# Hybrid attention layer on one core: the latent heads' gate projection as seven half-block products with tokens as rows

## The chip, the core and the metric

One core of a Trainium2 chip runs the whole layer in one launch. The time is the device time of an execution in microseconds. TensorE (PE) multiplies, VectorE (DVE) and ScalarE (ACT) work elementwise, GpSimd (POOL) and SyncE (SP) mostly issue DMAs here.

## The reference

512 tokens of width 2048, all in float32. The parts that matter:

```python
h = _rms_norm(x, g_pre)
proj = h @ w_in                      # split into q_lat, kv_lat, k_rope_raw, gate_mla, fq, fk, fv, f_logit, gate_fox
o_mla = _mla_branch(q_lat, kv_lat, k_rope_raw, g_q, w_uq, g_kv, w_ukv, cos, sin) * jax.nn.silu(gate_mla)
o_fox = _fox_branch(fq, fk, fv, f_logit, b_forget) * jax.nn.silu(gate_fox)
o = jnp.concatenate([o_mla, o_fox], axis=-1) @ w_out
return x + _rms_norm(o, g_post)
```

There are 8 latent (MLA) heads and 8 forgetting (fox) heads of width 128. gate_mla is the product of the normed x (512 x 2048) with a 2048 x 1024 block of w_in; it is this product that the change makes in another way.

## The kernel before

**Arithmetic.** Every operand of a product is split into a high and a low part, and `mm3` (L128 to 131) makes three matmuls of them: high x high (L129), high x low or low x high (L130, L131). x is turned at the start, so that its 16 blocks of 128 columns lie with columns on the partitions and 512 tokens in the row (`hh`, `hl`). The factor 1/rms of each token comes in later, as a row (`rrow`) or a column (`rcol`).

**Weights.** They come in chunks of 128 x 1024 numbers (512 KB). `load` (L205) issues a chunk's DMA on SP into one of three `raw` buffers. `divide` (L226) makes the parts: a cast on ACT (L232, tile whi) and a subtraction on DVE (L233, wlo), three buffers each. `chunk(i)` (L243) asks for loads four chunks ahead and divides two ahead. The list of chunks is in the order of use.

**Order of the work.** Projections run on TensorE chunk by chunk; a projection stage with weights as the stationary operand and 512 tokens moving is `proj_T` (L429), one with tokens as rows is `proj_V` (L442). After each block of 128 columns of x (a k step) `pump` takes a step from the queue `todo`: heads' scores, softmax, turns (L555) and values, operand splits and so on are worked off between projections. `drain` empties that queue. An order of each engine's instructions follows from this and from a scheduler, except for the first projection.

**Sums of weight blocks.** The output projection is already made, for each of two column pairs of 512, as seven products of half-sized blocks instead of eight (p1, p2, p4, q6, g5, g7, g3). These need sums of w_out's blocks (t4 to t7). `add_blocks` (L301) makes one with DMAs alone: a tiny mark DMA (L303), which waits for a divided chunk and so sets the time, a copy into DRAM on SP's queue (L305), and an accumulating DMA on POOL's queue (L306). The 32 sums are in `bg`; `behind` (L424) issues one every 8 k steps as soon as the first heads are done. The products also need sums of the heads' outputs: `operand_steps` (L853) makes and splits them (L867 on DVE, then L120 and L121), `put_away` (L896) writes six operands of each of two pairs to DRAM through POOL, but for a11 and a12, which stay, and `fetch` (L902) reads them back on SP in the output stage.

**Stages.** First forgetting pair, three more forgetting pairs (each with q, k, v, gate projections and the attention of the pair before in `todo`), the rotary tables in between; latents (loop L914, 10 blocks, times `rrow` by L920); latent gate (L976 to 994: four `proj_T` over 16 k steps, with `gate_of` L594: product with rrow L597, Tanh L598, product L599), in which the latents' norms are also made (`latent_squares` L926, `latent_scale` L939, whose row is made by TensorE at L408) and their parts split (`part_latents` L970); the MLA heads (loop L1000); the output stage (`product` L1130, from L1188).

A step of the products in the output stage, operand block stationary and weights moving:

```python
mm3(
    o[t], ah, al, hi[:, j, :], lo[:, j, :], first and kk == 0, last and kk == 7,
    skip_group_check=True,
)
```

Of the kernel before, what the change touches and what calls it, by code (L numbers as in the profile page):

```python
# [12 lines left out]
F32 = mybir.dt.float32  # L13
# [50 lines left out]
def tile_hybrid_layer(  # L64
# [26 lines left out]
    tp = inner.enter_context(tc.tile_pool(name="tp", bufs=3))  # L91
# [89 lines left out]
    half, dummy = (cst.tile([P, 1], F32, name=n) for n in ("half", "dummy"))  # L181
# [54 lines left out]
    state = {"loaded": 0, "divided": 0}  # L236
# [30 lines left out]
    gml = [add_chunks(w_in, [(0, O_GM + 256 * p, 256)], NK, 4, 256) for p in range(4)]  # L267
# [30 lines left out]
    W = {}  # L298
    bg = deque()

    def add_blocks(to, first, second, mark):  # L301

        nc.sync.dma_start(to[0:1, 0:16], mark)  # L303
        to = to.rearrange("p (k c) -> p k c", k=2)
        nc.sync.dma_start(to, first)  # L305
        pool.dma_start(to, second, accum_op=ALU.add)  # L306

    for g in range(2):
        for name in ("t7", "t6", "t4", "t5"):

            W[name, g] = [dr.tile([P, 1040], F32, name=f"{name}{g}{j}")[:, :1024] for j in range(4)]
        for j in range(4):
            b11, b12, b21, b22 = (out_block(k[j], 2 * g + c) for k in (K1, K2) for c in range(2))
            t7, t6 = (W[n, g][j].rearrange("p (k c) -> p k c", k=2) for n in ("t7", "t6"))
            for name, first, second in (("t7", b12, b22), ("t5", b11, b12), ("t6", b11, t7), ("t4", b21, t6)):
                bg.append(lambda mark, x=(W[name, g][j], first, second): add_blocks(*x, mark))

    def add_plain(pairs, c):
        first = len(chunks)
        for pair in pairs:  # L320
            add_chunks(w_out, [(0, 512 * c, 512)], 2, 2, 512, out_rows(pair) // P)
        return range(first, len(chunks))

    def add_sums(name, g):
        first = len(chunks)
        chunks.extend((W[name, g][j], None, 0, 2, 512) for j in range(4))
        return range(first, len(chunks))

    outp = {}
    for name, g in (  # L330
        ("p1", 0), ("p1", 1), ("p2", 0), ("p4", 0), ("p4", 1), ("q6", 0), ("g5", 0), ("g7", 0),
        ("q6", 1), ("g5", 1), ("g7", 1), ("g3", 0), ("g3", 1), ("p2", 1),
    ):
        plain = {"p1": (K1, 0), "p2": (K2, 0), "g3": (K2, 1)}
        sums = {"p4": "t4", "q6": "t6", "g5": "t5", "g7": "t7"}
        if name in plain:
            outp[name, g] = add_plain(plain[name][0], 2 * g + plain[name][1])
        else:
            outp[name, g] = add_sums(sums[name], g)
# [79 lines left out]

    def drain():  # L420
        while todo:
            todo.popleft()()

    def behind(k, w):  # L424

        if done and bg and k % 8 == 0:
            bg.popleft()(w[0:1, 0, 0:16].bitcast(F32))

    def proj_T(rng, outs, kh, kl, rate=1):  # L429

        k = 0
        n_k = sum(chunks[i][3] for i in rng)
        for i in rng:
            hi, lo = chunk(i)
            for j in range(chunks[i][3]):
                for o, rows, pick in outs:
                    mm3(o[:rows, :], pick(hi, j), pick(lo, j), kh[k], kl[k], k == 0, k == n_k - 1)
                k += 1
                pump(rate)
                behind(k, hi)  # L440

    def proj_V(rng, banks, kh, kl, rate=1):  # L442
# [3 lines left out]
        for i in rng:  # L446
            hi, lo = chunk(i)
            for j in range(chunks[i][3]):
# [9 lines left out]
                behind(k, hi)  # L458
# [266 lines left out]

    done = []
# [62 lines left out]

    for p in range(4):  # L790
# [57 lines left out]

    HALF = S // 2
    TERMS = ("a11", "a12", "a22", "q6", "g5", "g7", "g3")  # L850
    oper = {n: [None] * 4 for n in TERMS}

    def operand_steps(j, names, raw_of, place, then=None):  # L853

        a = {}
        raw = {}

        def block(n):
            if not a:
                for h, pair in ((1, K1[j]), (2, K2[j])):  # L860
                    for t in range(2):
                        a[f"a{t + 1}{h}"] = o_of[pair][:, :, t * HALF : (t + 1) * HALF]
            return raw[n] if n in raw else a[n]

        def make(n, x, y):
            raw[n] = raw_of(f"r{n}{j}").rearrange("p (h c) -> p h c", h=2)
            dve.tensor_tensor(out=raw[n], in0=block(x), in1=block(y), op=ALU.subtract)  # L867

        def part(n):
            both = place(f"s{n}{j}").rearrange("p x (h c) -> p x h c", h=2)  # L870
            split_into(both[:, 0], both[:, 1], block(n))
            oper[n][j] = both
            if then is not None:
                then(n, j)

        steps = []
        for n in names:
            if n == "sums":
                steps += [
                    lambda: make("g5", "a21", "a22"),  # L880
                    lambda: make("q6", "a11", "g5"),
                    lambda: part("g5"),
                    lambda: part("q6"),
                    lambda: make("g3", "a12", "q6"),
                    lambda: part("g3"),
                    lambda: make("g7", "a21", "a11"),
                    lambda: part("g7"),
                ]
            else:
                steps.append(lambda n=n: part(n))  # L890
        return steps

    kept = ("a11", "a12")
    away = {}

    def put_away(n, j):  # L896

        if n not in kept:
            away[n, j] = dr.tile([P, 1024], F32, name=f"away{n}{j}")
            pool.dma_start(away[n, j].rearrange("p (x h c) -> p x h c", x=2, h=2), oper[n][j].bitcast(F32))  # L900

    def fetch(n, j):  # L902
        both = slot(f"b{n}{j}", F32R)
        nc.sync.dma_start(both.bitcast(F32), away[n, j].rearrange("p (x c) -> p x c", x=2))
        oper[n][j] = both.rearrange("p x (h c) -> p x h c", h=2)

    for j in (1, 0):
        todo.extend(
            operand_steps(j, ("a11", "a12", "a22", "sums"), tmp, lambda n: slot(n, F32R), put_away)
        )  # L910


    raw = []
    for p in range(5):  # L914
# [9 lines left out]
    LAT = (("q", 0, 6, QR), ("k", 6, 10, KVR))  # L924

    def latent_squares():  # L926
        accs = []
        both = slot("ls")
        for j, (name, lo, hi, _) in enumerate(LAT):
            acc = both[:, j, :]  # L930
            for i in range(lo, hi):
                dst = acc if i == lo else tmp(f"lq{name}{i}")
                act.square(dst, raw[i])
                if i > lo:
                    pool.tensor_tensor(out=acc, in0=acc, in1=dst, op=ALU.add)
# [363 lines left out]
```

## Time and profile before

| | us |
|---|---|
| median of 3 runs | 923.75 (923.0 to 925.07) |
| profiled execution | 921.93 |
| its span | 920.1 |
| TensorE busy / DVE / ACT / POOL | 908.7 / 557.2 / 379.2 / 62.1 |
| DMA moved | 152.14 MB, mean 165 GB/s |

A row of groups reads: line, engine, operation, result <- inputs, number of instructions, busy time, mean ns of one, idle time of the engine before them and what ended it. Timeline rows start with the start in us from the span's begin and the length. TensorE's matmuls overlap in their records, so the distance of their starts says more than their length. Windows give the busy time of each engine in a stretch, then the granted clock of TensorE, the share of the 16 DMA engines and GB/s.

### The profile page before, as it was taken

The numbers are of one execution on the slowest core, as the hardware profiler recorded it, in microseconds if no ns is written. First come the engines' busy times: TensorE is split into PE (matmuls) and PEld (weight loads), VectorE is DVE, ScalarE is ACT, GpSimd is POOL, SyncE is SP. The second block draws the span as 40 slices with busy tenths as digits, with TensorE's granted clock in tenths as the row PEclk, the third lists the DMA queues.
The fourth block names the chain that finished last, engine by engine and source line by source line (L and its number), as shares of the span: only waits on it lengthen the run. The fifth ranks groups of instructions, "written<-read, shape, count | busy, mean of one in ns | idle before, by whom it ended". The sixth has DMA issues, their size and how long they took to land.

```text
span 920.1 us, 11945 instructions
## 1 busy us (share of the span) xinstructions
PE 908.7 (99%) x4472; PEld 771.3 (84%) x4472; DVE 557.2 (61%) x970; ACT 379.2 (41%) x683; POOL 62.1 (7%) x74
## 2 busy tenths in 40 slices
PE   8999999999999999999999999999999999999996
PEld 7888888998889888888888888888888888888885
DVE  3478744447833744483742234957978895876686
ACT  5772432233422522242421134434444455644473
POOL 1000000000000000000211013000000000000022
PEclk9999999999999999999999999999999999999999
DMA  9343365876666766766998733223222146787768
GB/s 303 90 116 114 92 160 138 209 181 180 150 159 173 197 168 153 197 167 162 293 279 211 177 92 92 81 82 96 57 63 84 46 138 209 241 318 230 274 194 249
DMA packets 109214, 152.14 MB, mean 165 GB/s; under 512 B 14274, under 2 KB 74204, under 8 KB 109156
## 3 DMA queue, kind: packets, MB, share of 16 engines
q1 hardware_dynamic: 99172, 126.86, 44.3%
q0 software_dynamic: 9248, 24.12, 14.1%
q8 instruction: 35, 0.57, 0.2%
q10 hardware_dynamic: 736, 0.40, 0.2%
q14 instruction: 23, 0.19, 0.1%
HBM read 141.90 MB, written 43.01 MB: 201 GB/s over the span
## 4 chain that ended last, share of the span: by engine, by line
PE 97%; DVE 2%; ACT 0%; issue 0%; DVEq 0%; ACTq 0%
PE fv L490 4%; PE l L129 4%; PE l L130 4%; PE l L131 4%; PE fg L129 3%; PE fq L129 3%; PE fq L130 3%; PE fq L131 3%; PE fg L130 3%; PE fg L131 3%; PE gm L129 3%; PE fk L129 3%; PE gm L131 3%; PE fk L130 3%; PE gm L130 3%; PE fk L131 3%
## 5 line engine op out<-in xcount | busy, mean ns | idle before, releaser
L233 DVE TENSOR_TENSOR wlo<-raw,whi 128x1024 fp32r<-128x1024 f32 (+3 forms) x181 | 215.6, 1193 | 231.3 <-ACT whi L232 223.3
L232 ACT CAST whi<-raw 128x1024 fp32r<-128x1024 f32 (+3 forms) x181 | 184.1, 1018 | 352.9 <-PE l L130 65.4
L129 PE MATMUL l<-h,whi 128*128 128x512 f32 x160 | 63.2, 395 | 0.0
L131 PE MATMUL l<-h,wlo 128*128 128x512 f32 x160 | 62.4, 390 | 0.0
L130 PE MATMUL l<-h,whi 128*128 128x512 f32 x160 | 62.3, 390 | 0.0
L129 PE MATMUL fq<-h,whi 128*128 128x512 f32 x128 | 52.7, 412 | 0.0
L129 PE MATMUL fg<-h,whi 128*128 128x512 f32 x128 | 50.4, 394 | 0.0
L130 PE MATMUL fq<-h,whi 128*128 128x512 f32 x128 | 50.2, 392 | 0.0
L131 PE MATMUL fq<-h,wlo 128*128 128x512 f32 x128 | 50.2, 392 | 0.0
L129 PE MATMUL fk<-h,whi 128*128 128x512 f32 x128 | 50.1, 391 | 0.0
L130 PE MATMUL fg<-h,whi 128*128 128x512 f32 x128 | 50.0, 390 | 0.0
L131 PE MATMUL fg<-h,wlo 128*128 128x512 f32 x128 | 49.9, 390 | 0.0
L129 PE MATMUL gm<-h,whi 128*128 128x512 f32 x128 | 49.9, 390 | 0.0
L131 PE MATMUL fk<-h,wlo 128*128 128x512 f32 x128 | 49.8, 389 | 0.0
L131 PE MATMUL gm<-h,wlo 128*128 128x512 f32 x128 | 49.8, 389 | 0.0
L130 PE MATMUL gm<-h,whi 128*128 128x512 f32 x128 | 49.8, 389 | 0.0
L130 PE MATMUL fk<-h,whi 128*128 128x512 f32 x128 | 49.8, 389 | 0.0
L131 PE MATMUL fv<-whi,h 128*128 128x256 f32 (+1 forms) x128 | 39.5, 309 | 0.0
L130 PE MATMUL fv<-wlo,h 128*128 128x256 f32 (+1 forms) x128 | 39.5, 309 | 0.0
L129 PE MATMUL fv<-whi,h 128*128 128x256 f32 (+1 forms) x128 | 39.5, 309 | 0.0
L306 POOL DMA_DIRECT2D t<-in_w_out_dram x16 | 18.7, 1169 | 293.6 <-DMA t<-in_w_out_dram 285.4
L490 PE MATMUL fv<-whi,h 128*128 128x456 f32 x128 | 37.9, 380 | 0.0
(401 smaller groups left out, 2086.4 us busy)
## 6 DMA issues: line engine op xcount, KB each, us to landing
raw<-in_w_in_dram SPq DMA_DIRECT2D x88, 512.0 KB
t<-in_w_out_dram SPq DMA_DIRECT2D x32, 512.0 KB
raw<-t SPq DMA_DIRECT2D x32, 512.0 KB
raw<-in_w_out_dram SPq DMA_DIRECT2D x24, 512.0 KB
t<-in_w_out_dram POOLq DMA_DIRECT2D x16, 512.0 KB, 7.0
t<-t POOLq DMA_DIRECT2D x16, 512.0 KB, 6.3
raw<-in_w_ukv_dram SPq DMA_DIRECT2D x8, 512.0 KB
xa<-in_x_dram SPq DMA_DIRECT2D x7, 512.0 KB
```

Of the source, the lines that this page charges most:

```text
L129: pe.matmul(o, ah, bh, start=first, stop=False, **kw)
L130: pe.matmul(o, ah, bl, start=False, stop=False, **kw)
L131: pe.matmul(o, al, bh, start=False, stop=last, **kw)
L232: act.copy(hi[:, :m], raw[:, :m])
L233: dve.tensor_tensor(out=lo[:, :m], in0=raw[:, :m], in1=hi[:, :m].bitcast(F32), op=ALU.subtract)
L306: pool.dma_start(to, second, accum_op=ALU.add)
L490: pe.matmul(banks[t][:, :n], a[k][:, tss[t]], b[:, j, :], start=k == 0 and m == 0, stop=k == NK - 1 and m == 2,)
```

## The change

The latent gate is made as seven products with tokens as rows, in the scheme of the output stage. The 512 tokens fall into two halves (x_block's `tokens` 0 and 2), the 2048 columns of x into two, the 1024 columns of the gate into two of 512. Each product has 8 k steps of 128 and two token tiles; x's block is the stationary operand, a divided chunk (two k steps of 512 columns) moves. p1, p4 and p2 take plain blocks of x, q6, g5, g7 and g3 take sums of blocks of x.

- Sums of w_in's gate blocks: 16 more `add_blocks`, at the head of `bg`. `behind` now counts k steps by a pace: every 6 with the forgetting heads, none in the latents (1000), every 2 in the MLA stage, where the k and v steps count too. The gate stage doesn't call it.
- Sums of x's blocks (`x_steps`): for each of four pairs, four DVE adds of high and low part, then `operand_steps` with "sums" (four subtractions, four splits); each result is put away to DRAM by POOL (16 put-aways). They are issued through `later`, one step every fourth k step, with the forgetting heads.
- The gate products fetch these 16 operands as they go: q6's four in p1, two of g5's in p4 and two in p2, g7's in q6, g3's in g5.
- The results are combined by `scaled` (DVE, with half of 1/rms as a column) and `scaled_copy` (ACT). `gate` turns them: 8 groups of four transposes of 128 x 128, Tanh on ACT straight from PSUM and one DVE product. Four groups stand in g3, four at the start of the MLA stage.
- a11 and a12 of the heads' pairs 0 and 1 are no longer kept, but put away (4 more) and fetched at the start of the MLA stage (4 more).
- Latents: ACT squares and scales by the gain from PSUM, in place of the DVE product with `rrow`; `latent_scale` is split, the q latents in the fourth latent projection, the k latents in p4. The rotary key moves into the latents' stage.
- Small: tp has four buffers instead of three, some small tiles are joined, the tile of the output's squares lies in another pool.

The core of the diff (the output stage keeps its products, through `add_products` and the same `product`):

```diff
-    gml = [add_chunks(w_in, [(0, O_GM + 256 * p, 256)], NK, 4, 256) for p in range(4)]
+    def gate_block(j, h, c):
+        k = 2 * j + 8 * h
+        return w_in[0, k * P : (k + 2) * P, O_GM + 512 * c : O_GM + 512 * (c + 1)].rearrange("(k p) c -> p k c", p=P)
+
+    sum_blocks("m", gate_block)
+    add_products(
+        [(n, "m") for n in ("p1", "p4", "p2", "q6", "g5", "g7", "g3")],
+        lambda g, h, c: add_chunks(w_in, [(0, O_GM + 512 * c, 512)], 8, 2, 512, 8 * h),
+    )
...
-    def behind(k, w):
-
-        if done and bg and k % 8 == 0:
-            bg.popleft()(w[0:1, 0, 0:16].bitcast(F32))
+    def behind(w):
+
+        if done and bg:
+            state["tiles"] += 1
+            if state["tiles"] >= state["pace"]:
+                state["tiles"] = 0
+                bg.popleft()(w[0:1, 0, 0:16].bitcast(F32))
+        if done:
+            state["turn"] += 1
+            if later and state["turn"] % 4 == 0:
+                later.popleft()()
...
+    def x_steps(j):
+
+        pair = [slot(f"xr{h}{j}") for h in range(2)]
+
+        def whole(h, i):
+            k = 2 * j + 8 * h + i
+            dve.tensor_tensor(out=pair[h][:, i, :], in0=hh[k].bitcast(F32), in1=hl[k].bitcast(F32), op=ALU.add)
+
+        for h in range(2):
+            for i in range(2):
+                whole(h, i)
+        later.extendleft(reversed(operand_steps("m", j, pair, ("sums",), tmp, part_slot, put_away)))
...
+    for j in range(4):
+        later.append(lambda j=j: x_steps(j))
...
-        for i in range(2):
-            t = both[:, i, :]
-            dve.tensor_tensor(out=t, in0=lb[i], in1=rrow, op=ALU.mult)
-            raw.append(t)
-    drain()
+        for i in range(2):
+            latent(2 * p + i, lb[i], both[:, i, :])
+        if p == 2:
+            wait(6)
+            todo.append(lambda: latent_scale(0))
+            wait(4)
+            todo.append(rotary_key)
...
-    for p in range(4):
-        gb = [proj_bank(f"gm{p}{i}") for i in range(2)]
-        if p == 3:
-            drain()
-            part_latents()
-        proj_T(gml[p], [(gb[i], P, two[i]) for i in range(2)], hh, hl)
-        both = slot(f"gm{p}")
-        o_of.append(both)
-        gm += [gate_of(gb[i], both[:, i, :], f"m{2 * p + i}") for i in range(2)]
+    def scaled(to, o, t0, add, op=ALU.add, col=hcol):
+
+        for t in range(2):
+            dve.scalar_tensor_tensor(
+                out=to[:, t, :], in0=o[t], scalar=col[:, t0 + t : t0 + t + 1], in1=add[:, t, :], op0=ALU.mult, op1=op
+            )
...
+    def gate(f, top, bottom):
+
+        if f % 2 == 0:
+            o_of.append(slot(f"gm{f // 2}"))
+        g = o_of[-1][:, f % 2, :]
+        pt = att_bank(f"gmt{f}")
+        c = slice(f % 4 * P, (f % 4 + 1) * P)
+        for t in range(NT):
+            pe.transpose(pt[:, t * P : (t + 1) * P], (top, bottom)[t // 2][:, t % 2, c], ident)
+        act.activation(g, pt, AF.Tanh)
+        dve.scalar_tensor_tensor(out=g, in0=g, scalar=1.0, in1=pt, op0=ALU.add, op1=ALU.mult)
+        gm.append(g)
+
+    wait(8)
+    todo.append(lambda: latent_scale(1))
+    A, B = ([proj_bank(f"g{n}{t}") for t in range(2)] for n in "ab")
+    product("p1", "m", x_block(0, 0), A, True, True, side=fetches("q6", "m"))
+    pa, pb = slot("gpa"), slot("gpb")
+    scaled_copy(pa, A, 0)
+    scaled_copy(pb, A, 2)
+    product("p4", "m", x_block(1, 2), B, True, True, side=fetches("g5", "m")[:2])
+    c21 = slot("gc21")
+    scaled(c21, B, 2, pb)
+    product("p2", "m", x_block(1, 0), A, False, True, side=fetches("g5", "m")[2:])
+    c11 = slot("gc11")
+    scaled_copy(c11, A, 0)
+    C = [proj_bank(f"gc{t}") for t in range(2)]
+    product("q6", "m", operand("q6", "m"), C, True, True, side=fetches("g7", "m"))
+    c12 = slot("gc12")
+    scaled(c12, C, 0, pa, ALU.subtract)
+    G = [proj_bank(f"gd{t}") for t in range(2)]
+    product("g5", "m", operand("g5", "m"), G, True, True, side=fetches("g3", "m"))
+    c22 = slot("gc22")
+    scaled(c22, G, 2, pb, ALU.subtract)
+    part_latents()
+    product("g7", "m", operand("g7", "m"), C, False, True)
+    todo.append(lambda: scaled(c21, C, 2, c21, col=ncol))
+    todo.append(lambda: scaled(c22, C, 2, c22))
+    for f in range(4):
+        todo.append(lambda f=f: gate(f, c11, c21))
+    product("g3", "m", operand("g3", "m"), G, False, True, 2)
+    drain()
+    todo.append(lambda: scaled(c12, G, 0, c12))
+    for f in range(4, 8):
+        todo.append(lambda f=f: gate(f, c12, c22))
+    state["pace"] = 2
+    for n in ("a11", "a12"):
+        for f in fetches(n, "o"):
+            f()
...
                 kk += 1
                 pump(2)
+                behind(hi)
```

More of the change, by code (lines that the diff above doesn't have):

```diff
@@ L180, in tile_hybrid_layer @@
     pool.memset(ones, 1.0)
-    half, dummy = (cst.tile([P, 1], F32, name=n) for n in ("half", "dummy"))
+    small = cst.tile([P, 2], F32, name="small")
+    half, dummy = small[:, 0:1], small[:, 1:2]
     chunks = []
@@ L318, in add_plain @@
[L318 to L339, printed above, removed]
+    for g in range(2):
+        sum_blocks(g, lambda j, h, c, g=g: out_block((K1, K2)[h][j], 2 * g + c))
@@ L788, in fox_v @@
             h += m
+    for j in range(4):
+        later.append(lambda j=j: x_steps(j))
     for p in range(4):
@@ L846, in tile_hybrid_layer @@
             make_gcol(gains2, NK, 10)
[L849 to L891, printed above, removed]
```

326 lines of the change are left out of this document (200 added, 126 removed).

## The prediction

> **What bounds the kernel now.** I read the page's busy times and the chain first, then TensorE's timeline in the stage that changes, then the windows by stage.
>
> ```profile
> span 920.1 us, 11945 instructions
> PE 908.7 (99%) x4472; PEld 771.3 (84%) x4472; DVE 557.2 (61%) x970; ACT 379.2 (41%) x683; POOL 62.1 (7%) x74
> PE 97%; DVE 2%; ACT 0%; issue 0%; DVEq 0%; ACTq 0%
> ```
>
> TensorE holds 97% of the chain that ends last, and no other engine passes 61%. So time goes only with TensorE instructions, or comes back as gaps between them. The busy time of one matmul is not its price, though:
>
> ```profile
> 530.24 0.39 PE L129 MATMUL gm<-h,whi 128*128 128x512 f32 x1
> 530.47 0.39 PE L130 MATMUL gm<-h,whi 128*128 128x512 f32 x1
> 530.69 0.39 PE L131 MATMUL gm<-h,wlo 128*128 128x512 f32 x1
> 530.92 0.39 PE L129 MATMUL gm<-h,whi 128*128 128x512 f32 x1
> ```
>
> Each shows 0.39 us, but the starts follow each other every (530.92 - 530.24)/3 = 0.227 us (0.2275 over longer stretches). That is what one more or one fewer costs. The stages, cut where the matmul's output tile changes name (pairs 2 to 4 of the forgetting heads, latents, latent gate, MLA heads, output):
>
> ```profile
> 124.00:408.00 284.00, 284.00 (x1449) 244.32 (x1448) 150.32 (x291) 90.09 (x158) 22.37 (x22) 1.00 0.70 173
> 408.00:523.00 115.00, 115.00 (x524) 95.22 (x523) 49.79 (x63) 32.71 (x44) 15.21 (x20) 1.00 0.83 228
> 523.00:613.00 90.00, 90.00 (x406) 74.62 (x405) 50.08 (x75) 36.46 (x56) 11.27 (x8) 1.00 0.32 92
> 613.00:745.00 132.00, 131.94 (x746) 114.80 (x745) 108.62 (x214) 62.50 (x132) 0.00 (x0) 1.00 0.25 71
> 745.00:913.00 168.00, 166.55 (x763) 137.89 (x761) 120.95 (x185) 92.52 (x146) 9.49 (x10) 1.00 0.73 237
> ```
>
> Columns: window, its length, busy time of PE, weight load, DVE, ACT, POOL, then clock, DMA share, GB/s. TensorE is full in all five, at clock 1.00. DVE and ACT have room everywhere on average; DMA has room in the gate and MLA stages, less in the others.
>
> **The change: what TensorE loses and gains.** The gate projection's matmuls:
>
> ```profile
> L129 PE MATMUL gm<-h,whi 128*128 128x512 f32 x128 | 49.9, 390 | 0.0
> ```
>
> Three forms of 128 make 384 (L130 and L131 have as many). The new products make 7 x 8 k steps x 2 token tiles x 3 = 336. In these the x block is the stationary operand and the weights move, as in the output stage:
>
> ```profile
> 805.26 0.39 PE L129 MATMUL ob<-whi,ba 128*128 128x512 f32 x1
> 805.49 0.39 PE L130 MATMUL ob<-wlo,ba 128*128 128x512 f32 x1
> 805.71 0.39 PE L131 MATMUL ob<-whi,ba 128*128 128x512 f32 x1
> ```
>
> Same spacing, so 48 x 0.2275 = **-10.9 us**. The gate must then be turned: 8 groups of 4 transposes of 128x128. The nearest row is a group of the heads:
>
> ```profile
> 138.03 0.60 PE L555 MATMUL ptf<-ident,pf 128*128 128x128 f32 x4
> 138.38 0.47 PE L129 MATMUL fq<-h,whi 128*128 128x512 f32 x1
> 138.70 0.40 PE L130 MATMUL fq<-h,whi 128*128 128x512 f32 x1
> ```
>
> The group takes 0.35 us until the next start, and that next matmul takes 0.32 instead of 0.23: 0.44 a group, 8 x 0.44 = **+3.5 us**. The latents' small matmuls are regrouped, not multiplied. Net on TensorE: **-7.4 us**. The rest is whether gaps open.
>
> **Added beside TensorE, forgetting stage.** For each of four pairs of x blocks: 4 adds, 4 subtractions and 4 splits (one ACT cast, one DVE subtract each), on 128x512 or two of these.
>
> ```profile
> L121 DVE TENSOR_TENSOR sg<-rg,sg 128x512 fp32r<-128x512 f32 x12 | 8.2, 684 | 1.3 <-ACT sg L120 1.3
> L120 ACT CAST sg<-rg 128x512 fp32r<-128x512 f32 x12 | 7.2, 601 | 3.5 <-DVE rg L867 2.6 <-DVE rq L867 0.8
> L233 DVE TENSOR_TENSOR wlo<-raw,whi 128x1024 fp32r<-128x1024 f32 x152 | 187.6, 1236 | 198.2 <-ACT whi L232 190.6 <-PE sm L529 4.0 <-DMA raw<-in_w_out_dram 1.5
> L232 ACT CAST whi<-raw 128x1024 fp32r<-128x1024 f32 x152 | 159.8, 1052 | 312.1 <-PE l L130 65.4 <-PE fk L130 41.1 <-PE fq L130 39.9
> ```
>
> DVE gets 4 x 12 x 0.69 = 33 us on 150.3 of 284, ACT 16 x 0.60 = 9.7 on 90.1. They come one at a time, every fourth k step, and weights are divided two chunks ahead (a chunk here is 24 matmuls = 5.46 us, so 10.9 us ahead, less the 1.05 + 1.24 of the divide). That hides a 0.7 us instruction; without that cover each would cost its 0.7 us, 42 us in all, far from any sign of the trace. One stretch is already full:
>
> ```profile
> 230.00:253.00 23.00, 23.00 (x114) 19.15 (x113) 20.28 (x32) 9.74 (x15) 1.99 (x2) 1.00 0.61 151
> 460.00:483.00 23.00, 23.00 (x103) 19.06 (x102) 9.48 (x11) 5.10 (x6) 3.37 (x5) 1.00 0.98 279
> ```
>
> There (rotary tables) DVE is busy 20.3 of 23 us; three or four more instructions (2.7 us) fill it just.
>
> DMA. One block sum is a copy on SP's queue and an accumulate on POOL's, 0.52 MB each; one put-away is a POOL write of 0.52 MB.
>
> ```profile
> q1 hardware_dynamic: 99172, 126.86, 44.3%
> q0 software_dynamic: 9248, 24.12, 14.1%
> t<-in_w_out_dram POOLq DMA_DIRECT2D x16, 512.0 KB, 7.0
> t<-t POOLq DMA_DIRECT2D x16, 512.0 KB, 6.3
> awayg<-sg POOLq DMA_DIRECT2D x6, 512.0 KB, 8.4
> ```
>
> 44.3% of 920 us for 126.9 MB is 3.2 us of all engines per MB, 14.1% for 24.1 MB is 5.4; a sum takes 1.7 + 2.8 = 4.5 us. Counted in the changed order, the stage issues 29 sums instead of 22 (one every 6 k steps), and 16 put-aways: 7 x 4.5 + 16 x (1.7 to 2.8) = 58 to 76 us over 284, share 0.70 -> 0.91 to 0.97. The window 460:483 above ran at 0.98 with TensorE full, so a full DMA alone opens no gap. What can: a slot whose put-away has not landed.
>
> ```profile
> 440.77 0.60 POOL L900 DMA_DIRECT2D awaya<-sa  x1 [2.54 <-DVE sa L121]
> 446.64 0.62 ACT L120 CAST sa<-gf 128x512 fp32r<-128x512 f32 x1 [2.07 <-DMA awaya<-sa]
> ```
>
> ACT stood 2.07 us for a put-away issued 5.9 us earlier; TensorE lost nothing. In the changed order (places counted in matmuls of 0.2275 us), at about 281 us, ACT's split for an operand is to reuse a slot some 3.4 us after that slot's put-away goes out behind an accumulate. At 8.4 us landing, ACT (with the divides queued behind it, and TensorE behind these) stands about 5 us, where the cover is 8.6 less what ACT has queued. Bounds 0 (as in the row) to 5; near the row, **+1.2 us**.
>
> **Gate stage.** A chunk now feeds 12 matmuls, 2.73 us instead of 5.46: 28 chunks for 16. DVE +12 x 1.24 = 14.8, ACT +12 x 1.05 = 12.6, on 50.1 and 36.5 of 90; DVE also combines results (the 8 gate products with the row of norms go, 12 scaled sums of about 0.69 come). Two chunks ahead are now 5.5 us, less 2.3 of divide: **cover about 3 us**. The output stage lives on the same:
>
> ```profile
> 783.70 1.05 ACT L232 CAST whi<-raw 128x1024 fp32r<-128x1024 f32 x1 [1.82 <-PE oa L131]
> ```
>
> There ACT waits for TensorE to free a buffer, not for a load: divides run ahead as far as they can. Three things could eat 3 us. (a) The second latents' norm now ends inside p4; TensorE makes its row when its chain is done. Now the chain takes:
>
> ```profile
> 568.11 0.70 PE L945 MATMUL lb<-ones,ls 128*128 128x1 f32 x5
> 574.70 0.40 PE L408 MATMUL lrq<-lrqdh,ones 128*128 128x512 f32 x1
> ```
>
> 6.6 us, for two latents. In the new order TensorE has about 30 matmuls, 6.9 us, between the two places, and three divides stand between: 0 to 1.5, I take **0.6**. (b) The transposes wait for sums that DVE makes after a product ends (4 x 0.69 = 2.8 us and one divide of 1.24, against 18 matmuls = 4.1 us): 0 to 1, I take **0.3**. (c) Loads: p1, q6 and g5 fetch one 0.52 MB operand per chunk beside its own 0.52 MB, 1.05 MB per 2.73 us = 385 GB/s; over p1 to g5, 20 loads and 16 fetches, 18.9 MB in 54.6 us = 346. What the output stage reaches:
>
> ```profile
> 825.00:830.00 5.00, 5.00 (x23) 4.13 (x22) 2.79 (x3) 1.67 (x3) 0.00 (x0) 1.00 0.96 355
> ```
>
> and, from 805 to 828 in 40 slices,
>
> ```profile
> GB/s 392 420 406 378 427 399 406 271 14 171 313 370 86 0 107 214 399 235 235 249 306 342 378 385 385 392 406 385 356 363 292 235 328 420 363 313 378 385 385 420
> ```
>
> Seven slices running, at 378 to 427, are about the need: **0.3**, bounds 0 and the first rival's price. In the Trainium skill, "DMA: Bandwidth & Descriptors", section "Specifications", the HBM limit of one core is put at about 358 GB/s. By that 1.05 MB would take 2.93 us, 0.20 more than a chunk gives, 12 x 0.20 = 2.4 us in the three products, of which the cover would take most (an estimate from that page). The slices above 378 speak against it for a core that runs alone.
>
> The stage's slack in ACT and DVE hides the rest: squares and gains taken straight from PSUM in the latents' stage (ACT 32.7 of 115), the rotary key moved there.
>
> **MLA stage.** 19 sums instead of none: 19 x 4.5 = 86 of 132 us, share 0.25 -> 0.90, and four 0.52 MB fetches on SP's queue ahead of the first weight loads (2.1 MB at 355 to 400 GB/s, 5 to 6 us). The first divides come with the second half of the gate's combining still on DVE, and four transposes wait for a sum after only 9 matmuls (2.05 us against 1.4 of DVE). Bounds 0 and 3; **+0.8 us**. Sums still land 60 us before the product that needs them.
>
> **Sum.** -10.9 + 3.5 + 1.2 + 0.6 + 0.3 + 0.3 + 0.8 = -4.2 us. Against the profiled execution (921.93 us: span 920.1 and 1.83 around it) this is 917.7; the median of the runs, 923.75, lies 1.82 above that execution, so **919.5**.
>
> **Rivals.**
> 1. *The gate stage becomes bound by its loads (slower).* Three raw buffers go round every 3 x 2.73 = 8.2 us; less ACT's 1.05, DVE's 1.24 and about 0.5 of issue, a load may take 5.4 us. Over 20 chunks that is 7 rounds: stall = 7 x (L - 5.4) - 3 of cover. For L there is only a neighbour: a copy of the same size on the same queue
>
> ```profile
> 134.07 0.57 SPq L305 DMA_DIRECT2D t<-in_w_out_dram  x1
> ...
> 139.06 1.14 POOL L306 DMA_DIRECT2D t<-in_w_out_dram  x1 [9.94 <-DMA t<-in_w_out_dram]
> ```
>
> landed within 5.0 us, for; accumulates take 7.0, against. At L = 7.0: 8.2 us in place of 0.3, 927.4. It makes the kernel slower (over 925.6) from L = 6.75. Chance 0.15.
> 2. *Put-aways hold the forgetting stage (no change).* With DMA at 0.95 each of the four pairs blocks ACT beyond the cover by about 1.5 us, the stretch of the rotary tables among them: 6 in place of 1.2, 924.3; at 1 us each 922.3. For: the 2.07 us wait at a lower DMA share; against: that wait cost TensorE nothing. 0.18.
> 3. *All is covered*: -7.4, 916.4. For: every stage shows a full TensorE, even at DMA 0.98. 0.16.
> 4. *The products cost more per matmul than they save*: at 0.25 us each 336 x 0.0225 = 7.6, 927.1. Against: the output stage's spacing. 0.03.
>
> **How the numbers follow.** Forecast 0.48 (918 to 921.8). A measurement tells 0.2% from no change, so faster is below 921.9 and slower above 925.6: faster 0.48 + 0.16 = 0.64, same 0.18, slower 0.15 + 0.03 = 0.18. The range goes from 915.8 (rival 3 with a little gained where DVE work left) to 927.0 (rival 2 and most of rival 1), leaving out about 0.15.
>
> **What would show it.** Gate stage: 336 matmuls at 0.2275 and 8 groups of about 0.44, stage 79 to 81 us to the last product (now 90); ACT waits there for TensorE, not for loads. Latents' stage unchanged at 115. Forgetting stage 284 to 286, DMA share over 0.9. MLA stage 134 to 135 with four of the turnings. Output stage as now, 168. Wrong if ACT's divides in p1, q6 or g5 wait for a DMA on raw (rival 1), or ACT for "away" around 280 with TensorE idle (rival 2), or MLA's first chunks come over 3 us late.

## The result, and the profile after

The changed kernel takes 933.96 us (median of 6 runs, 931.31 to 938.62) against 923.75 (6 runs, 922.89 to 925.07): ratio 1.0118, 95% interval 1.009 to 1.0146. It is slower by some 10 us, where 4.2 us less was forecast. The profiled execution, 931.31, is the fastest of the six.

The page of the changed kernel, the rows that answer to those of before:

```profile
span 929.4 us, 12266 instructions
PE 906.9 (98%) x4456; PEld 768.4 (83%) x4456; DVE 595.6 (64%) x1034; ACT 407.6 (44%) x730; POOL 89.3 (10%) x110
PE 88%; DMA 7%; DVE 2%; ACT 1%; SPq 1%; issue 0%; DVEq 0%; POOL 0%; ACTq 0%; POOLq 0%
```

TensorE is busy 1.8 us less, but its part of the chain that ended last falls from 97% to 88%, and DMA, which was not in the chain, has 7% of it. The same stages as before, cut at the same matmuls:

```profile
124.00:416.00 292.00, 286.70 (x1449) 245.60 (x1448) 178.45 (x339) 98.59 (x174) 38.57 (x45) 0.99 0.87 223
416.00:533.00 117.00, 117.00 (x536) 96.96 (x535) 55.46 (x79) 45.02 (x70) 16.20 (x21) 1.00 0.47 156
533.00:612.00 79.00, 79.00 (x361) 65.16 (x360) 53.35 (x71) 43.85 (x58) 2.53 (x2) 1.00 0.83 277
612.00:753.00 141.00, 136.40 (x764) 118.00 (x763) 109.94 (x216) 62.94 (x134) 18.75 (x19) 0.99 0.92 228
753.00:919.00 166.00, 166.00 (x761) 137.63 (x759) 120.05 (x183) 91.30 (x143) 7.84 (x9) 1.00 0.74 238
```

From the first matmul of each stage to the first of the next (timeline of TensorE), in us:

| stage | before | after | difference |
|---|---|---|---|
| forgetting pairs 2 to 4 | 284.1 | 292.1 | +8.0 |
| latents | 115.0 | 116.5 | +1.5 |
| latent gate | 89.9 | 79.8 | -10.1 |
| MLA | 132.0 | 140.6 | +8.6 |
| output, to the last matmul | 165.9 | 165.8 | 0 |
| after the last matmul | 8.9 | 10.6 | +1.7 |

So the part that was rebuilt got faster, as worked out, and two stages in which TensorE computes what it did before (but for four turnings, 1.8 us, in the MLA stage) got slower. (The last row is the landing of the last store; the engines' steps there have the same lengths as before.) What TensorE waited for (after the colon: us in all, times, longest):

```profile
PE fv L129 <- ACT whi L233: 3.1, 1, 3.1
PE ptm L585 <- ACT pm L576: 1.8, 1, 1.8
PE mq L129 <- DVE mk L121: 1.3, 1, 1.3
...
PE sm L559 <- ACT pm L576: 1.2, 1, 1.2
```

The waits are few, and those shown are behind ACT or DVE. What held these engines shows in the chain (start, length, what the chain passes through). In the forgetting stage:

```profile
274.29 3.54 DMA t<-whi
...
277.85 7.58 DMA t<-in_w_out_dram
...
286.69 9.38 DMA awaymg<-smg
...
296.70 0.84 ACT whi L233
```

Read from below: the divide that TensorE needs (whi) stands behind ACT's split (smq), which waits for a put-away (9.38 us to land); POOL could issue that only at 286.69, behind an accumulate that waited for the copy of its weight sum (7.58 us), which waited on SP for its mark (3.54). At the start of the MLA stage the marks are slow themselves:

```profile
613.23 7.01 DMA t<-whi
620.25 0.57 SPq L277
620.87 2.86 DMA t<-whi
...
630.29 5.79 DMA t<-whi
```

A mark moves 0.1 KB; it took 7.01 us. SP, in order, stands at a copy until its mark has landed, and what comes later waits:

```profile
SPq L277 <- DMA t<-whi: 19.7, 7, 7.6
```

That is from 612 to 700: 19.7 us in all, 7 times, the longest 7.6. SP's queue behind the third of the marks above:

```profile
630.29 1.48 SPq L275 DMA_DIRECT2D t<-whi  x3
636.11 1.23 SPq L277 DMA_DIRECT2D t<-in_w_out_dram  x2
637.43 2.25 SPq L221 DMA_DIRECT2D raw<-in_w_ukv_dram  x2
```

Two weight loads go out at 637.43, after SP had stood 4.3 us (631.77 to 636.11). In this profile TensorE does not wait for these two. It waits in three places of the stage. At 640.0 (1.33 us) ACT's divide stood behind the mark of 5.79 us, with the split of mk queued behind it. At 660.6 (1.82 us) the softmax was queued behind a divide that waited for TensorE itself; why it came so late was not followed. At 691.3 (1.24 us) the softmax was queued behind a divide that waited for one weight load of the third pair:

```profile
678.77 8.48 DMA raw<-in_w_ukv_dram
687.35 1.06 ACT whi L233
...
690.55 0.68 ACT pm L576 x2
691.28 0.74 PE sm L559 x4
```

A gap also costs more than itself. Around the one at 294 (the clock is the third number from the end):

```profile
294.00:298.00 4.00, 0.86 (x4) 0.31 (x2) 1.13 (x2) 1.82 (x3) 0.19 (x1) 1.00 0.53 206
298.00:301.00 3.00, 2.44 (x9) 2.43 (x9) 2.25 (x3) 0.99 (x2) 0.35 (x1) 0.62 0.69 211
301.00:304.00 3.00, 3.00 (x16) 3.00 (x15) 0.00 (x0) 0.00 (x0) 0.00 (x0) 0.81 0.99 296
640.00:643.00 3.00, 3.00 (x8) 2.42 (x9) 2.40 (x5) 1.56 (x4) 0.80 (x1) 0.51 1.01 277
```

After it the granted clock is 0.62 and 0.81 for six us. The stage's gap of some 4 us (3.1 and 0.6) became 5.8: the v projection there went from 33.9 to 39.7. In the MLA stage (last row) the clock was 0.51 for three us after the wait at 640, which was only 1.33 us. The mean clock of the six runs was 0.989 to 0.993, against 0.998 in the profiled execution before.

### The profile page after: what moved, and what is told of

It is laid out like the page before. It is cut to its first block, busy times and chain, and to the rows that moved or that the text cites. A ratio compares the mean times of both kernels' runs of the same rounds, so it can differ in the third digit from the quotient of the medians.

```text
span 929.4 us, 12266 instructions
## 1 busy us (share of the span) xinstructions
PE 906.9 (98%) x4456; PEld 768.4 (83%) x4456; DVE 595.6 (64%) x1034; ACT 407.6 (44%) x730; POOL 89.3 (10%) x110
## 4 chain that ended last, share of the span: by engine, by line
PE 88%; DMA 7%; DVE 2%; ACT 1%; SPq 1%; issue 0%; DVEq 0%; POOL 0%; ACTq 0%; POOLq 0%
PE fv L520 4%; PE l L129 4%; PE l L131 4%; PE l L130 4%; PE fq L131 3%; PE fq L129 3%; PE fq L130 3%; PE fk L130 3%; PE fk L129 3%; PE fk L131 3%; PE fg L129 3%; PE fg L130 3%; PE fg L131 3%; PE sm L559 2%; DMA t<-whi 2%; PE sf L559 2%
## 5 line engine op out<-in xcount | busy, mean ns | idle before, releaser
L234 DVE TENSOR_TENSOR wlo<-raw,whi 128x1024 fp32r<-128x1024 f32 (+3 forms) x193 | 228.2, 1185 | 192.7 <-ACT whi L233 187.3
L233 ACT CAST whi<-raw 128x1024 fp32r<-128x1024 f32 (+3 forms) x193 | 196.7, 1021 | 284.6 <-PE fk L130 54.7
L131 PEld LDWEIGHTS l<-h,wlo 128*128 128x128 f32 x160 | 30.0, 188 | 6.5
L129 PEld LDWEIGHTS l<-h,whi 128*128 128x128 f32 x160 | 30.1, 188 | 5.9
L130 PEld LDWEIGHTS l<-h,whi 128*128 128x128 f32 x160 | 30.1, 188 | 5.8
```

The lines of the kernel that those rows point to most:

```text
L129: pe.matmul(o, ah, bh, start=first, stop=False, **kw)
L130: pe.matmul(o, ah, bl, start=False, stop=False, **kw)
L131: pe.matmul(o, al, bh, start=False, stop=last, **kw)
L233: act.copy(hi[:, :m], raw[:, :m])
L234: dve.tensor_tensor(out=lo[:, :m], in0=raw[:, :m], in1=hi[:, :m].bitcast(F32), op=ALU.subtract)
```

## The experiments

Theory 1 (T1): transfers do it, the put-aways in the forgetting stage and the weight sums in the MLA stage. T2: the added work of DVE and ACT, and what moved to the start of the MLA stage. T3: SP's queue, standing at copies. Stage times are those of one profiled execution each; the median, and its ratio to runs of the kernel before on the same chip, is what counts for the whole.

**e1, fewer sums in the MLA stage.**

```diff
-    for g in range(2):
+    for g in range(1):
         sum_blocks(g, lambda j, h, c, g=g: out_block((K1, K2)[h][j], 2 * g + c))
...
-            if name in blocks:
-                plain(g, *blocks[name])
+            if name in blocks or g == 1:
+                plain(g, *blocks.get(name, (0, 0)))
```

> Leaves out the 16 sums of w_out for the second column pair: those products read plain blocks of the same size, so the output is not the layer's. Nearly all sums that the changed kernel issues in the MLA stage are gone (3 of 19 stay), all else is as changed. Stages of the profiled changed kernel: forgetting pairs 2 to 4 292.1 us, latents 116.5, gate 79.8, MLA 140.6 (before: 284.1, 115.0, 89.9, 132.0). Theory T1 (the sums' transfers hold the MLA stage): MLA 133.7 to 135.5 (132.0 plus four turnings of 0.44, plus up to 1.7), whole time 6 us below the changed kernel's, forgetting stage unchanged within 3 us. Rival T2 (the fetches of a11 and a12 and the gate's combining, which also moved to the start of this stage): MLA stays above 138.5.

It takes 927.25 us, ratio 1.0035 (1.0014 to 1.0057), where the changed kernel has 1.0118. MLA takes 135.1, the forgetting stage 294.2. This is as T1 had it: 5.5 of the 6.9 us that the MLA stage lost beyond its turnings go with the sums.

**e2, no put-aways in the forgetting stage.**

```diff
     def put_away(n, of, j):
 
+        if of == "m" and (n, j) != ("g5", 0):
+            away[n, of, j] = away["g5", "m", 0]
+            return
```

> Leaves out 15 of the 16 put-aways of x's sums (the fetches all read the one that is left, so the gate is wrong): no POOL writes in the forgetting stage but the sums, and no slot held by a landing; DVE's and ACT's work on x's sums stays, and so do the 29 weight sums. T1 (put-aways hold slots and load the DMA engines): forgetting stage 292.1 -> 284.5 to 287, whole time about 6 us below the changed kernel's. T2 (the added DVE and ACT instructions, or the 7 added weight sums, hold the stage): it stays at 289.5 or more. MLA stage unchanged at 138 to 142 in both.

It takes 932.31 us, ratio 1.0098 (1.0079 to 1.0118). The gap at 294 is gone (that projection is back at 33.87), but the stage stays at 292.6: other gaps take its place. The third pair's q projection, with the rotary tables, loses 4.9 us against before, and the fourth pair 3.6; in the changed kernel each lost 1.1. So T1 in this form is wrong, and T2 as the expectation words it, with the seven more sums in it, holds. The chain of this kernel at the largest gap:

```profile
221.74 0.56 SPq L277
222.36 9.46 DMA pos<-in_positions_dram
231.84 0.43 DVE ang L724
232.26 0.61 DVE plf L121
```

The load of the positions for the rotary tables, on SP right behind a sum's copy, took 9.46 us; DVE stood for it, with the attention's split (plf) queued behind. In the fourth pair it was the load of the heads' rows nk, 7.96 us.

**e3, the sums spread as before the change.**

```diff
-    state = {"loaded": 0, "divided": 0, "tiles": 0, "turn": 0, "pace": 6}
+    state = {"loaded": 0, "divided": 0, "tiles": 0, "turn": 0, "pace": 8}
...
-    state["pace"] = 1000
+    state["pace"] = 6
...
-    state["pace"] = 2
+    state["pace"] = 3
```

> The whole computation; only the pace of weight sums is changed: every 8th k step with the forgetting heads (22 sums, as before), every 6th in the latents (13, where the changed kernel issues none), every 3rd in the MLA stage (13 instead of 19). T1: MLA 140.6 -> 136 to 138 (the loss goes with the number of sums), forgetting stage 292.1 -> 288 to 290, latents 116.5 to 118 at a DMA share near 1; whole time 6 to 8 us below the changed kernel's, about 926. Rival (what holds the forgetting stage is the put-aways alone): that stage stays above 291. Rival T2 for MLA: above 139.

It takes 926.31 us, ratio 1.0035 (1.0016 to 1.0053): the expected time, but not by the expected way. The forgetting stage is at 284.2, against 284.1 before, with all put-aways and all DVE and ACT work of x's sums in it: at this pace that work costs nothing, which refutes T2 there. MLA is at 133.6, also better than expected. But the latents went to 125.4:

```profile
493.66 1.16 POOL L278 DMA_DIRECT2D t<-in_w_out_dram  x1 [10.75 <-issue]
494.40 3.92 POOL L1032 TENSOR_TENSOR ls<-ls,lq 128x512 f32<-128x512 f32 x2
```

POOL adds the latents' squares, and its queue is in order: the additions stood behind an accumulate before which POOL was idle for 10.75 us (the profile names nothing that ended this wait), and TensorE waited 5.67 us for the sum.

**e4, marks and copies on POOL's queue.**

```diff
-        nc.sync.dma_start(to[0:1, 0:16], mark)
+        pool.dma_start(to[0:1, 0:16], mark)
         to = to.rearrange("p (k c) -> p k c", k=2)
-        nc.sync.dma_start(to, first)
+        pool.dma_start(to, first)
```

> The whole computation; the mark and the copy of each weight sum are issued on POOL's queue instead of SP's. The same bytes move. Theory T3 (SP's queue stands at a copy until its mark has landed, up to 7.6 us, and weight loads are issued late behind it): MLA falls to 134 to 136. Rival T1 as bandwidth (the engines are full, whoever issues): MLA stays at 138 to 142. In the forgetting stage put-aways now stand behind marks and copies on POOL, so by T1 that stage grows to 294 or more; by T3 it falls by 2 to 3.

It takes 1036.54 us, ratio 1.1221 (1.1202 to 1.124). The forgetting stage takes 351.0 and MLA 184.4, far beyond either expectation. What ACT waited for:

```profile
ACT whi L233 <- DMA t<-whi: 76.7, 12, 10.7
...
ACT smg L120 <- DMA awaymg<-smg: 32.2, 2, 17.8
```

A mark reads a divided chunk, and ACT may not write the next chunk there until it has landed. On POOL's queue the marks stood behind accumulates, so the divides did too. T3 is not tested cleanly by this, since it moves the hold from SP to ACT; it shows what a late mark costs.

**e5, e3 with the additions on DVE.**

```diff
-            pool.tensor_tensor(out=acc, in0=acc, in1=dst, op=ALU.add)
+            dve.tensor_tensor(out=acc, in0=acc, in1=dst, op=ALU.add)
```

> The whole computation: e3's paces (8 / 6 / 3), and the additions of the latents' squares on DVE instead of POOL, so that they don't stand behind the accumulating DMAs on POOL's queue (in e3 TensorE waited 5.67 us for one of them and the latents' stage took 125.4 us). Theory now (the loss is where the weight sums are issued, not their number nor x's sums): forgetting stage 284.2 to 285, latents 116.5 to 117.5, gate 79.8, MLA 133.5 to 134.5; sum of the four 6 to 7 us below before's 621.0, whole time 916.5 to 918.5, ratio about 0.993. Rival (a full DMA in the latents' stage, share 0.9, delays loads there by itself): latents stay at 120 or more and the time is 921 or more.

It takes 920.57 us, 918.05 to 925.52, ratio 0.9995 (0.998 to 1.001): no difference from before that can be told. The forgetting stage (284.2) and the latents (117.4) are as expected; the gate (82.0) and MLA (138.5) are not. The chain in the MLA stage:

```profile
632.87 9.53 DMA raw<-in_w_ukv_dram
...
642.50 1.06 ACT whi L233
```

One weight load took 9.53 us, and ACT, at its divide, had the softmax behind it.

**e6, the kernel before with 19 sums in its MLA stage** (paces 13, none and 2).

```diff
-        if done and bg and k % 8 == 0:
-            bg.popleft()(w[0:1, 0, 0:16].bitcast(F32))
+        if done and bg:
+            state["tiles"] += 1
+            if state["tiles"] >= state["pace"]:
+                state["tiles"] = 0
+                bg.popleft()(w[0:1, 0, 0:16].bitcast(F32))
...
                 kk += 1
                 pump(2)
+                behind(kk, hi)
```

> The kernel before, whole computation; only its 32 weight sums are paced as in the changed kernel's last part: every 13th k step with the forgetting heads (13), none in the latents, every 2nd in the MLA stage (19). Theory (19 sums at this pace hold the MLA stage by themselves): MLA 132.0 -> 137 to 140, forgetting stage 284 and latents 115 or a little less, whole time 5 to 8 us above before. Rival (the changed kernel's MLA stage is slow for its four turnings, its four extra fetches and the combining at its start): MLA stays below 133.5 and the time within 2 us of before.

It takes 923.54 against 921.78, ratio 1.0015 (1.0005 to 1.0025). The MLA stage:

```profile
615.00:747.00 132.00, 131.94 (x747) 114.84 (x745) 108.77 (x214) 62.93 (x133) 17.53 (x18) 1.00 0.90 218
```

131.9 us at a DMA share of 0.90 and TensorE full. The expected loss did not come: 19 sums alone do not make it.

**e7, the kernel before with a sum every 6th k step.** The edit of e6, with the pace 6 throughout:

```diff
-    state = {"loaded": 0, "divided": 0}
+    state = {"loaded": 0, "divided": 0, "tiles": 0, "pace": 6}
```

> The kernel before, whole computation; only the pace of its weight sums is changed to every 6th k step (29 with the forgetting heads instead of 22, 3 in the latents). No x sums, no put-aways in that stage. If the pace of the sums alone holds the forgetting stage: 284.1 -> 287 to 293 and the time 3 to 8 us above before. Rival (it takes the put-aways and x's work beside them): forgetting stage below 285.5, time equal to before within 2 us.

It takes 926.21 us, ratio 1.0039 (1.0024 to 1.0054); the forgetting stage is 287.05, the lower edge of what the first theory gave. The gap is e2's, the positions' load (8.78 us) behind a copy. So the denser pace alone costs the stage 2.9 us.

**e8, e5 with a sum every 6th k step with the forgetting heads** (and every 12th in the latents).

```diff
-    state = {"loaded": 0, "divided": 0, "tiles": 0, "turn": 0, "pace": 8}
+    state = {"loaded": 0, "divided": 0, "tiles": 0, "turn": 0, "pace": 6}
...
-    state["pace"] = 6
+    state["pace"] = 12
```

> The whole computation: as e5, but every 6th k step with the forgetting heads (29 sums instead of 22) and every 12th in the latents (6 instead of 13); the MLA stage has 13 in both. Theory (7 more sums beside the 16 put-aways hold the forgetting stage): forgetting stage 289 to 295 against e5's 284 to 285, all else as e5, time 5 to 9 us above e5. Rival (the loss there is a matter of chance from run to run, or of what comes later): within 2 us of e5.

It takes 927.26 us, ratio 1.0064 (1.0049 to 1.0079). The forgetting stage of e8, then of e5:

```profile
124.00:415.00 291.00, 285.28 (x1448) 244.16 (x1448) 178.63 (x340) 98.62 (x175) 38.59 (x45) 1.00 0.86 223
```

```profile
124.00:408.00 284.00, 283.77 (x1448) 244.21 (x1448) 178.66 (x339) 98.83 (x174) 32.05 (x38) 1.00 0.78 203
```

The same engine work, seven more sums on POOL (45 against 38 instructions), DMA share 0.86 against 0.78, and 6.8 us. So it is the seven more sums that turn this stage from 284.2 to 291.0, but not alone: without x's sums and put-aways they cost 2.9 us (e7), with x's sums but no put-aways 8.5 (e2).

**e9, the changed kernel with a11 and a12 fetched ahead of the last MLA pair.**

```diff
-    for n in ("a11", "a12"):
-        for f in fetches(n, "o"):
-            f()
...
     for p in range(4):
+        if p == 3:
+            for n in ("a11", "a12"):
+                for f in fetches(n, "o"):
+                    f()
         c = mla[p]
```

> The whole computation: the changed kernel with one edit, the four fetches of a11 and a12 (2.1 MB on SP's queue) are issued ahead of the last of the four MLA pairs instead of ahead of the first. In e6 19 sums at the same pace cost the MLA stage nothing (131.9 us) where there were no fetches, turnings or combining at its start; in e1 the stage took 135.1 with fetches and 3 sums; in the changed kernel, with both, 140.6. Theory (the backlog that fetches and sums make together delays weight loads at the start of the stage): MLA 140.6 -> 134 to 136, forgetting stage as in the changed kernel (290 to 294), time 4 to 6 us below it, 928 to 930. Rival (turnings and combining beside the sums, or the sums themselves now that DVE is fuller): MLA stays at 138 or more.

In the profile MLA fell to 135.0 as expected, but the median is 932.98 (927.94 to 936.66; ratio 1.0132, 1.0114 to 1.0149), not 928 to 930: the profiled execution was the fastest, and what it shows need not hold for the others. Nothing gained that can be told.

**e10, e5 with the edit of e9.**

> The whole computation: e5 (paces 8 / 6 / 3, additions on DVE) with the fetches of a11 and a12 ahead of the last MLA pair. In e5 the MLA stage took 138.5 because one weight load landed 9.5 us after its issue. Theory: MLA 133.5 to 134.5, the rest as in e5 (284.2, 117.4, 80 to 82), time 916.5 to 919. Rival (late loads come from 13 sums wherever the fetches are): MLA 136 or more, 920 or more.

It takes 918.91 us, 917.2 to 922.5, ratio 0.9972 (0.9961 to 0.9983): a little faster than before. The forgetting stage takes 284.3, the latents 118.2, the gate 79.8, MLA 134.1.

**e11, e10 with paces 8 / 8 / 2** (10 sums in the latents, 16 in the MLA stage).

```diff
-    state["pace"] = 6
+    state["pace"] = 8
...
-    state["pace"] = 3
+    state["pace"] = 2
```

> The whole computation: as e10, but every 8th k step in the latents too (10 sums) and every 2nd in the MLA stage (16). Theory (the MLA stage carries 16 sums once the fetches are gone from its start, as before's carried 19 in e6; and the gate stage, which in e5 ran from load to load and took 82.0, gets a shorter backlog from the latents): latents 116.5 to 117, gate 79.8 to 80.5, MLA 133.5 to 135, time 915.5 to 918. Rival (sums in MLA cost by their number beside turnings and combining): MLA 136 or more and the time above e10's.

It takes 920.26 us, 916.52 to 929.0, ratio 0.9987 (0.9966 to 1.0007). The latents (116.5) and the gate (79.8) are as expected, MLA (139.8) is not. SP's queue and ACT in this stage (which begins at 604.5):

```profile
631.23 0.55 SPq L277 DMA_DIRECT2D t<-in_w_out_dram  x1
631.88 1.08 SPq L221 DMA_DIRECT2D raw<-in_w_ukv_dram  x2
```

```profile
640.07 1.04 ACT L233 CAST whi<-raw 128x1024 fp32r<-128x1024 f32 x1 [4.94 <-DMA raw<-in_w_ukv_dram]
```

The two loads of the second pair's w_ukv chunks go out 27.4 us into the stage, behind a copy that waited for its mark; ACT then stood 4.94 us for the first. It is the place of e5's gap too. Into the stage, these loads were issued at 22.9 us in e10 (stage 134.1), 23.5 in e1 (135.1), 24.1 in e9 (135.0), 24.6 in e3 (133.6), 25.0 in the changed kernel (140.6), 25.4 in e5 (138.5), 26.2 in e8 (136.0); in e6 at 21.6, with no loss. The order is not strict: e3 lost nothing at 24.6, and the waits of the changed kernel were not for these loads.

**e12, e11 without the second column pair's sums** (e1's edit): no sums in the MLA stage.

> Leaves out the 16 sums of w_out for the second column pair (those products read plain blocks of the same size, so the output is not the layer's): as e11, 22 sums with the forgetting heads, 10 in the latents, none in the MLA stage, whose only added DMAs are the four late fetches. Theory (what is left of the loss in e10 and e11, and their spread of 5 and 12 us from run to run, is weight loads that land late beside sums in the MLA stage): MLA 133.6 to 134.2 (132.0 and four turnings), time 914.5 to 917, all runs within 3 us. Rival (turnings, combining and DVE's fuller stage make it): MLA 136 or more or a spread as in e11.

It takes 916.24 us, 915.23 to 916.86, ratio 0.9927 (0.9909 to 0.9945); its output is not the layer's. MLA takes 133.8, and the four runs lie within 1.6 us. Turnings, combining and late fetches cost no more than their matmuls, and the narrow spread points to the sums for that of e11 too.

**e13, e10 with no sums in the first MLA pair.**

```diff
-    state["pace"] = 3
+    state["pace"] = 1000
...
     for p in range(4):
+        if p == 1:
+            state["pace"] = 2
```

> The whole computation: as e10, but no weight sum is issued during the first of the four MLA pairs; its 13 sums come every 2nd k step in the other three. In the profiles so far the place that stalls is one: ACT's divides of the two w_ukv chunks of the second pair, whose loads SP issued 22.9 us into the stage in e10 and e12 (stage 134.1, 133.8), 25.0 to 27.4 in e5, e8, the changed kernel and e11 (136.0 to 140.6), behind copies that wait for their marks. Theory (this one place, loads issued late behind sums and landing slowly beside them, is the loss): loads issued by 23, MLA 133.6 to 134.4, time 916 to 918, spread under 4 us, ratio about 0.994. Rival (13 sums at a denser pace in three pairs meet the next pairs' loads in the same way): MLA 136 or more in the profile, or a median above e10's 918.9 with as wide a spread.

It takes 918.08 us, 917.16 to 918.94, ratio 0.9951 (0.9937 to 0.9965): the best version of the whole computation, 4 us below before. SP's queue, and the whole stage:

```profile
628.00 1.87 SPq L221 DMA_DIRECT2D raw<-in_w_ukv_dram  x2
```

```profile
605.00:740.00 135.00, 135.00 (x767) 117.22 (x766) 111.05 (x217) 64.51 (x138) 12.73 (x13) 1.00 0.75 194
```

The place that the expectation names stalls in e5, e9 and e11; the changed kernel's three waits are elsewhere, as shown above. Here the loads go out 22.8 us into the stage, TensorE is full, the stage is 133.8, and the five runs lie within 1.8 us of each other. It has the same 13 sums as e5 and e10, in other places: the place counts, and not the number alone. Against e10 the profiles differ by only 0.3 us in this stage; the gain shows in the ratio (0.9951 against 0.9972, with intervals that just overlap) and in the spread.

## Why the prediction was wrong

**TensorE's own sum was right.** Forecast: -10.9 for the products, +3.5 for the turnings. Latents and gate together (the small matmuls of the norms moved from one to the other) went from 204.9 to 196.2, -8.7; with the four turnings that stand in the MLA stage (4 x 0.44 = 1.8) -6.9, for -7.4. The rows of the turnings, from the chain:

```profile
606.22 0.44 PE gmt L1112 x4
608.05 0.44 PE gmt L1112 x4
```

0.44 a group, as taken from the heads' turns. In the whole, e13 has 614.9 us in the four stages against before's 621.0, -6.1.

**The gate stage's stalls were small, as forecast, and rival 1 did not come.** Forecast was +1.2. The stage's 336 matmuls, four turnings, and the norm's small matmuls (0.79 + 2 x 0.23) make 79.5 of its 79.8. Loads beside fetches were fast enough for TensorE, but not for ACT, which was to wait for TensorE only:

```profile
ACT whi L233 <- DMA raw<-in_w_in_dram: 2.7, 1, 2.7
ACT whi L233 <- DMA raw<-t5m: 1.8, 1, 1.8
ACT whi L233 <- DMA raw<-t6m: 1.8, 1, 1.8
```

TensorE stood for none of these 6.3 us. The rival was not far off: in e5, whose chain there runs from load to load (4.4 to 6.3 us each), the stage took 82.0.

**The failed step of the forgetting stage** is "+1.2 us" for put-aways that hold slots. The place was right (forecast at 281, the chain above shows the split at 296 waiting for the put-away issued at 286.7), the size was not: 5.8 us at that place alone, the slowed clock among it, and 8.0 in the stage. The cause was named only in part. With the sums every 8th k step the same put-aways cost nothing (e3, e5: 284.2) or little (286.0 in e12's profile); with the put-aways gone and the sums every 6th, the stage takes 292.6 (e2). It is the seven more sums, beside the work of x's sums (e7, e2), which meet put-aways and also single loads (positions, the heads' rows nk). The prediction had the seven sums only as DMA share, and for the single loads no term. Rival 2, the same mechanism, was priced at 6 where 8.0 was measured; it had no more for the MLA stage than the forecast, so its 924.3 fell short too.

**The failed step of the MLA stage** is "+0.8 us, bounds 0 and 3": measured 6.9 (8.6 less the four turnings). I had raised the DMA share from 0.25 to 0.90 (0.92 measured) and cost it at nearly nothing, because "a full DMA alone opens no gap". That was read from one window of the latents' stage. It is true there, and in e6 even in the MLA stage. But that row says nothing of an engine that stands behind a late transfer. In the changed MLA stage SP's copies stood for their marks, single transfers took 5.8 to 8.5 us, and ACT's divides, with splits and softmax queued behind them, held TensorE; one of the three waits, at 660.6, was not traced to a transfer. Against e12, which has no sums in this stage, the changed kernel is 5.2 us behind when the second pair's k projection starts (51.5 against 46.3 us into the stage) and 6.8 at the end. In e5 and e11 there is mainly one gap, in the same part of the stage, at the w_ukv loads of the second pair. That the sums do it shows e1, where 5.5 of the 6.9 us go with them, and the median with them (ratio 1.0035 for 1.0118); that their place counts shows e13, whose stage with 13 sums takes e12's 133.8. By which transfer a gap comes differs from kernel to kernel.

**What stays open.** Why e6 carried 19 sums in this stage without that gap: its loads were issued earlier (21.6), but whether the change's fetches, turnings or only another order of SP's queue moved them by 1 to 6 us was not taken apart; e9, which moved the fetches alone, gained nothing in its median. How the six runs of the changed kernel come to lie up to 7 us apart was not profiled; that e12 and e13, without gaps in that stage, lie within 2 us speaks for gaps that come or not. Part of the spread arises earlier, though: among the profiles the second forgetting pair begins at 123.8 (e8) to 127.3 us (e3). The 1.7 us after the last matmul were not looked into.

## What to carry to other kernels

Background transfers cost time here where something in order stood behind them. Before raising their pace, list for each stage the single loads that share their issue queue, the engine that waits for each, and what is queued behind that engine; the marks and put-aways belong on that list. The share of DMA time does not tell it: in the MLA stage 0.90 cost nothing in one order (e6), and about 0.75 cost 5 us in one (e5) and nothing in another (e13). When work is moved into a stage, take the evidence that it is hidden from that stage, with its own chunk time and queues, and look at the spread of the runs as well as at one profile.

## What the runs showed of the hardware

- After a wait of 3.14 us on TensorE the granted clock fell to about half for a few us (0.62 and 0.81 on average in the windows above; matmuls of 384 columns followed each other every 0.32 us in the timeline, where 384/512 of 0.2275 is 0.17), and after one of 1.33 us in the MLA stage to 0.51. In the Trainium skill, "TensorE: Matmul & The Clock Gate", section "What's actually happening", the clock drops to half after an idle window of 3413 ns, whose start is free-running. The trace agrees on the halving; but both waits here were shorter than that window, while one of 2.9 us at the same place in e8 left the clock of its stage at 1.00. So the length of a wait alone does not tell it.
- A DMA of 0.1 KB took 7.0 us to land and a 0.5 MB load 8.5 in the changed kernel's MLA stage, and such a load 9.5 in that of e5; loads in e5's gate stage took 4.4 to 6.3.
- An accumulating DMA at the head of POOL's queue held POOL's additions too: in e3 POOL was idle for 10.75 us before it, and with the additions on DVE (e5) the latents' stage went from 125.4 to 117.4 us.
